# Where the decay broadcasts of an SSD scan are issued: from SyncE's DMA queue or from GpSimd's

## The chip, the cores and the metric

One core of one Trainium2 chip runs the whole program. The metric is the device time of one execution in microseconds (us); the kernel before has a median of 3172.28 us over three runs (3169.02 to 3177.87). Engines are called as in the profile: PE (TensorE), DVE (VectorE), ACT (ScalarE), POOL (GpSimd) and SP (SyncE). SP does no arithmetic here; in the kernel before it issues every DMA of the program.

## What is computed

The reference is one layer of a hybrid decoder for 2048 prompt tokens and 8 x 4 sample tokens, all in float32. A wide input projection feeds a depthwise convolution branch (31 taps) and a Mamba-2 SSD branch with 32 heads in 8 groups, chunks of 128 tokens and a state of 128; the branches are gated, projected, merged and projected again. What bears on the change is the SSD scan of one chunk:

```python
cum = jnp.cumsum(dtc * a, axis=2)                      # per head, over the chunk's 128 tokens
seg = cum[:, :, :, None] - cum[:, :, None]
decay = jnp.exp(jnp.where(mask, seg, -jnp.inf))        # 128 x 128 per head
cb = jnp.einsum('bcqgn,bckgn->bcqkg', cc, bc)
y_intra = jnp.einsum('bcqkgr,bckgrp->bcqgrp', cb[..., None] * decay, xdt)
...
y_inter = jnp.einsum('bcqgn,bcgrpn->bcqgrp', cc, h_starts) * jnp.exp(cum)[..., None]
```

For the difference `seg` on the chip, a token's cumulative sum has to stand on all 128 partitions (as a row) as well as in its own (as a column).

## The kernel before

Pass 1 (from line 900 on) does the input projection, the short convolutions, the 31-tap convolution and the SSD scan; pass 2 the output projections. Pass 1 goes over the tokens in two halves: the first has 1024 prompt tokens and the 32 sample tokens in three token blocks of 352, the second 1024 prompt tokens in two of 512. In each half the loop runs over 88 weight blocks of 1024 x 128. A float32 product is made of three matmuls (`mm3`, lines 134 to 140), so one weight block takes 24 matmuls per token block. The raw weights are loaded by `load_raw` (line 120, two buffers), split by ACT (line 130) and DVE (line 131) into two parts (three buffers each), and the products are accumulated in one of four PSUM tiles called `acc`, from which ACT or DVE empties them (`evac`, from line 759 on; line 768 for the blocks that feed the SSD branch).

The SSD work is put between these blocks. A unit is one group of four heads and one chunk: 8 groups x 9 units in the first half (the ninth holds the sample tokens) and 8 x 8 in the second. Each block-and-token-block step of the loop is a tick; a unit takes three ticks (two in places), and the small units of PE, ACT and DVE work are emitted at fixed ticks:

- `ssd_prefetch` (lines 594 to 606) takes one of five `se` tiles and loads into it the four heads' negated cumulative sums, broadcast to all 128 partitions (line 602; 128 x 4 x 128 floats, 256 KB; a ninth unit has three smaller loads, lines 602 and 606). Their source is the scratch tensor `d_cum`, written at line 535. It is called for the first three waiting units at the start of each unit (`prefetch(3)` in `tick_pre`), and for the first two of a group when that group is made.
- `ssd_seg` (lines 608 to 624) has ACT make the differences (line 621, four per unit) and the exponentials (line 623).
- `ssd_a_pe` and `ssd_a_vec` transpose and multiply on PE (lines 643 to 649) and DVE (lines 662 to 672); `ssd_b_pe` has PE read `se` for the last time (lines 706 and 709), and with that the tile is free.

POOL has small work only: the rows that a convolution needs from the block before it (lines 547, 548, 550, 859 to 862), the same for the 31-tap convolution (lines 876, 878, 891, 897), and a few sample-token steps (lines 655, 738, 875, 893).

The order of each engine's instructions is made by the tile framework, which takes the emitted order and the priorities given (`high_priority`); it may put an instruction earlier than it was emitted. Each engine, and each DMA-issuing queue, works its instructions off in that order: one that waits holds up all behind it.

Of the kernel before, what the change touches and what calls it, by code (L numbers as in the profile page):

```python
# [13 lines left out]
P = 128  # L14
# [73 lines left out]
class Kernel:  # L88
# [505 lines left out]
    def ssd_prefetch(self, un):  # L594
        if un is None:
            return
        half, g, c = un["half"], un["g"], un["c"]
        se = self.se_tile()
        un["se"] = se
        w, q0 = (P, c * P) if c < 8 else (NH, HALF)  # L600
        src = self.D["cum"][half][4 * g:4 * g + 4, q0:q0 + w]
        self.Q.dma_start(se[:, 0:4, :w], src.rearrange("(o h) q -> o h q", o=1).to_broadcast([P, 4, w]))
        if c < 8:
            return
        for r in range(2):
            self.Q.dma_start(se[64 * r:64 * r + 64, 4:6, :w], src[r:4:2].rearrange("(o h) q -> o h q", o=1).to_broadcast([64, 2, w]))

    def ssd_seg(self, un):

# [825 lines left out]
```

## Time and profile before

| what | value |
|---|---|
| median of three runs | 3172.28 us |
| the profiled execution | 3171.67 us, of which the profile's span is 3169.9 us |
| busy: PE, DVE, ACT, POOL | 3121.7, 2292.6, 1604.9, 145.3 us |
| DMA traffic | 392.92 MB, all of the program's own on one queue |
| DMA issues at lines 602 and 606 | 136 and 16, all on SP |

The span is the time from the first to the last instruction of the profiled execution. An engine's busy time leaves out waiting, and it leaves out the issuing of DMAs, which the profile keeps apart as the engine's sequencer (SPq, POOLq). A row of the waits names the instruction that waited, the one that released it, the total time, the number of times and the longest.

### The profile page before, as it was taken

The page shows a single profiled execution, that of the slowest core. Times are in us where ns is not written, and L with a number is a line of the kernel's source. Part 1 is how long each engine was busy: PE and PEld are TensorE (multiplying, and loading weights), DVE is VectorE, ACT ScalarE, POOL GpSimd, SP SyncE. Part 2 cuts the span into 40 slices and gives each one's busy share as a digit, 9 for nine tenths or more (in the row PEclk, how much of TensorE's full clock was granted, in tenths as well). Part 3 has the DMA queues.
Part 4 walks back from the last instruction along what each step waited for, and adds up shares of the span by engine and source line. Part 5 has one row for each costly group of instructions (what it writes and reads, how often), then busy time and mean ns, then how long its engine had stood idle before and what let it go on. Part 6 is the DMA issues. An engine that isn't in the chain of part 4 may idle for free.

```text
span 3169.9 us, 46695 instructions
## 1 busy us (share of the span) xinstructions
PE 3121.7 (98%) x18404; PEld 2801.7 (88%) x18404; DVE 2292.6 (72%) x3350; ACT 1604.9 (51%) x2515; POOL 145.3 (5%) x266
## 2 busy tenths in 40 slices
PE   7999999999999999999999999999999999999997
PEld 5999999999999999787778778777778999999997
DVE  5798796968779684477776957859557877777654
ACT  5765545545464533655644646456425553535332
POOL 0000010100001000000000000000000000000000
PEclk9999999999999999999999999999999999999999
DMA  5533333233333343222222222332327767666752
GB/s 215 158 96 107 84 94 94 80 105 90 89 86 93 99 137 119 79 60 87 83 74 78 81 81 79 102 93 67 97 92 251 228 198 248 210 227 214 229 162 88
DMA packets 235563, 392.92 MB, mean 124 GB/s; under 512 B 31568, under 2 KB 171280, under 8 KB 234320
## 3 DMA queue, kind: packets, MB, share of 16 engines
q1 hardware_dynamic: 235344, 389.94, 40.2%
q8 instruction: 144, 2.36, 0.3%
q14 instruction: 75, 0.61, 0.1%
HBM read 314.66 MB, written 75.22 MB: 123 GB/s over the span
## 4 chain that ended last, share of the span: by engine, by line
PE 92%; DMA 3%; DVE 3%; ACT 2%; issue 1%; SPq 0%; POOL 0%; ACTq 0%; DVEq 0%; POOLq 0%
PE acc L138 27%; PE acc L140 27%; PE acc L139 27%; PE ys L706 2%; PE ys L714 2%; DMA se<-d_cum 2%; PE ys L709 2%; PE tr L649 1%; DMA set<-xT 1%; PE tr L300 1%; PE tr L643 1%; PE tr L645 0%; PE tr L644 0%; ACT se L621 0%; DMA d_hx<-set 0%
## 5 line engine op out<-in xcount | busy, mean ns | idle before, releaser
L138 PE MATMUL acc<-hh,wh 128*128 128x352 f32 (+1 forms) x3520 | 1268.3, 360 | 0.0
L140 PE MATMUL acc<-hh,wl 128*128 128x352 f32 (+1 forms) x3520 | 1234.2, 351 | 1.0 <-DVE wl L131 1.0
L139 PE MATMUL acc<-hl,wh 128*128 128x352 f32 (+1 forms) x3520 | 1234.1, 351 | 0.0
L138 PEld LDWEIGHTS acc<-hh,wh 128*128 128x128 f32 x3520 | 661.5, 188 | 66.3 <-issue 3.9
L140 PEld LDWEIGHTS acc<-hh,wl 128*128 128x128 f32 x3520 | 661.1, 188 | 63.1 <-DVE wl L131 1.3
L139 PEld LDWEIGHTS acc<-hl,wh 128*128 128x128 f32 x3520 | 661.9, 188 | 60.5 <-issue 0.7
L584 DVE SCALAR_TENSOR_TENSOR acc<-u,cwh,acc 128x1024 f32<-128x1024 f32 x480 | 614.7, 1281 | 5.4
L130 ACT ACTIVATE wh<-wr 128x1024 fp32r<-128x1024 f32 x336 | 354.9, 1056 | 492.3 <-PE acc L139 455.8
L131 DVE TENSOR_TENSOR wl<-wr,wh 128x1024 fp32r<-128x1024 f32 x336 | 410.0, 1220 | 261.1 <-ACT wh L130 259.1
L621 ACT ACTIVATE se<-se,cum 128x128 f32<-128x128 f32 x544 | 176.9, 387 | 495.2 <-DMA se<-d_cum 461.0
L553 DVE SCALAR_TENSOR_TENSOR set<-raw,prm,set 128x1080 f32<-128x1080 f32 (+1 forms) x192 | 250.8, 1306 | 4.2 <-ACT set L545 2.9
L662 DVE TENSOR_TENSOR se<-se,set 128x512 f32<-128x512 f32 x120 | 82.4, 687 | 223.9 <-ACT se L623 220.9
L138 PE MATMUL acc<-yh,wh 128*128 128x416 f32 x640 | 226.2, 353 | 0.0
L140 PE MATMUL acc<-yh,wl 128*128 128x416 f32 x640 | 225.9, 353 | 0.0
L139 PE MATMUL acc<-yl,wh 128*128 128x416 f32 x640 | 223.4, 349 | 0.0
L623 ACT ACTIVATE se<-se 128x1024 f32<-128x1024 f32 (+1 forms) x136 | 135.1, 993 | 2.2 <-DMA se<-d_cum 0.2
L139 PEld LDWEIGHTS acc<-yl,wh 128*128 128x128 f32 x640 | 120.3, 188 | 2.9 <-issue 1.0
L623 ACT ACT_TABLE_LOAD x95 | 121.9, 1283 | 1.7
L138 PEld LDWEIGHTS acc<-yh,wh 128*128 128x128 f32 x640 | 120.1, 188 | 1.7 <-issue 1.0
L140 PEld LDWEIGHTS acc<-yh,wl 128*128 128x128 f32 x640 | 120.0, 187 | 0.8
L138 PE MATMUL acc<-mh,wh 128*128 128x416 f32 x320 | 114.1, 357 | 0.0
L706 PE MATMUL ys<-se,xd 128*64 128x128 f32 x1088 | 113.5, 282 | 0.0
(259 smaller groups left out, 3900.3 us busy)
## 6 DMA issues: line engine op xcount, KB each, us to landing
wr<-win SPq DMA_DIRECT2D x176, 512.0 KB
wr<-wso SPq DMA_DIRECT2D x80, 512.0 KB
se<-d_cum SPq DMA_DIRECT2D x128, 256.0 KB
wr<-wco SPq DMA_DIRECT2D x40, 512.0 KB
wr<-wo SPq DMA_DIRECT2D x40, 512.0 KB
yy<-d_y SPq DMA_DIRECT2D x40, 416.0 KB
tm<-d_m SPq DMA_DIRECT2D x80, 208.0 KB
d_m<-sp SPq DMA_DIRECT2D x48, 176.0 KB
```

Of the source, the lines that this page charges most:

```text
L130: self.S.activation(out=hi[:, :cols], in_=raw[:, :cols], func=AF.Copy)
L131: self.V.tensor_tensor(out=lo[:, :cols], in0=raw[:, :cols], in1=hi[:, :cols].bitcast(F32), op=ALU.subtract)
L138: self.PE.matmul(out, whi[:, w], hhi(k), start=first and k == 0, stop=False)
L139: self.PE.matmul(out, whi[:, w], hlo(k), start=False, stop=False)
L140: self.PE.matmul(out, wlo[:, w], hhi(k), start=False, stop=last and k == KD - 1)
L553: V.scalar_tensor_tensor(out=acc, in0=raw[:, k:k + L], scalar=w[:, k:k + 1], in1=acc, op0=ALU.mult, op1=ALU.add)
L584: V.scalar_tensor_tensor(out=a, in0=u[:, k:k + HALF], scalar=w[:, k:k + 1], in1=a, op0=ALU.mult, op1=ALU.add)
L621: self.S.activation(out=se[:, m + h, :w], in_=se[:, h, :w], func=AF.Relu, bias=col)
L623: self.S.activation(out=se[:, a:b, :w], in_=se[:, a:b, :w], func=AF.Exp, scale=-1.0)
L662: V.tensor_tensor(out=se[:, 0:4], in0=se[:, 0:4], in1=bc(un["C"], "p (o q) -> p o q", [P, 4, P], o=1), op=ALU.mult)
L706: PE.matmul(ys[64 * r:64 * r + 64, b * P:b * P + w], xd[:w, 2 * b + r, :], un["m"][:w, 2 * b + r, :w], start=True, stop=not inter)
L709: PE.matmul(ys[64 * r:64 * r + 64, b * P:b * P + w], self.hT[:, g, 64 * h:64 * h + 64], se[:, h, :], start=False, stop=True)
```

## The change

The three loads in `ssd_prefetch` are issued by `self.G` (`nc.gpsimd`, POOL) where `self.Q` (`nc.sync`, SP) issued them. Source, destination, size and callers stay as they are.

```diff
@@ -599,11 +599,11 @@
         un["se"] = se
         w, q0 = (P, c * P) if c < 8 else (NH, HALF)
         src = self.D["cum"][half][4 * g:4 * g + 4, q0:q0 + w]
-        self.Q.dma_start(se[:, 0:4, :w], src.rearrange("(o h) q -> o h q", o=1).to_broadcast([P, 4, w]))
+        self.G.dma_start(se[:, 0:4, :w], src.rearrange("(o h) q -> o h q", o=1).to_broadcast([P, 4, w]))
         if c < 8:
             return
         for r in range(2):
-            self.Q.dma_start(se[64 * r:64 * r + 64, 4:6, :w], src[r:4:2].rearrange("(o h) q -> o h q", o=1).to_broadcast([64, 2, w]))
+            self.G.dma_start(se[64 * r:64 * r + 64, 4:6, :w], src[r:4:2].rearrange("(o h) q -> o h q", o=1).to_broadcast([64, 2, w]))
```

## Rows read from the trace of the kernel before

**Rows 1.** The page, parts 0 and 1: span, busy time and share.

```profile
span 3169.9 us, 46695 instructions
PE 3121.7 (98%) x18404; PEld 2801.7 (88%) x18404; DVE 2292.6 (72%) x3350; ACT 1604.9 (51%) x2515; POOL 145.3 (5%) x266
```

**Rows 2.** Windows of the two SSD stretches: length, then busy time of each engine.

```profile
160.00:1200.00 1040.00, 1031.57 (x7217) 983.15 (x7216) 822.57 (x1308) 539.01 (x964) 74.39 (x155) 1.00 0.35 96
...
1320.00:2320.00 1000.00, 996.36 (x5306) 792.70 (x5305) 728.89 (x1035) 544.09 (x822) 51.64 (x71) 1.00 0.28 83
```

**Rows 3.** PE's longest wait in 160 to 1200 and in 1310 to 2310.

```profile
PE ys L744 <- DVE set L735: 5.5, 6, 1.1
...
PE ys L321 <- ACT sp L337: 2.0, 2, 1.5
```

**Rows 4.** The tile `se`: its loads (duration ns min/median/max, first and last start).

```profile
L602 SPq DMA_DIRECT2D se<-d_cum x136: 359/377/2904, 136.8 to 2290.8; - x136
...
L606 SPq DMA_DIRECT2D se<-d_cum x16: 599/640/1441, 218.1 to 1161.5; - x16
```

**Rows 5.** Waits of SP's queue, whole span: total, times, longest.

```profile
SPq L120 <- DVE wl L131: 1024.2, 268, 23.2
...
SPq L602 <- PE ys L709: 107.1, 59, 9.9
```

**Rows 6.** Timeline of SP's queue, first half: start, length, instruction.

```profile
442.34 0.39 SPq L602 DMA_DIRECT2D se<-d_cum  x1
...
468.46 0.36 SPq L602 DMA_DIRECT2D se<-d_cum  x1
...
536.98 9.88 SPq L602 DMA_DIRECT2D se<-d_cum  x2
...
580.58 0.90 SPq L602 DMA_DIRECT2D se<-d_cum  x1
```

**Rows 7.** Timeline of PE around one load, first half.

```profile
468.03 0.39 PE L709 MATMUL ys<-se,hT 128*64 128x128 f32 x4
...
472.56 0.32 PE L140 MATMUL acc<-hh,wl 128*128 128x352 f32 x1
...
486.39 0.32 PE L138 MATMUL acc<-hh,wh 128*128 128x352 f32 x1
...
504.35 0.41 PE L138 MATMUL acc<-hh,wh 128*128 128x352 f32 x1
```

**Rows 8.** Timeline of ACT behind the same load, first half (in brackets: idle before).

```profile
473.29 1.28 ACT L621 ACTIVATE se<-se,cum 128x128 f32<-128x128 f32 x4 [4.62 <-DMA se<-d_cum]
...
476.85 0.45 ACT L768 ACTIVATE raw<-acc 128x352 f32<-128x352 f32 x1
...
480.01 1.06 ACT L130 ACTIVATE wh<-wr 128x1024 fp32r<-128x1024 f32 x1
```

**Rows 9.** Waits of ACT, whole span: the one on these loads.

```profile
ACT se L621 <- DMA se<-d_cum: 461.0, 114, 8.6
```

**Rows 10.** POOL's groups of instructions: busy, mean ns, then idle before and releasers.

```profile
L860 POOL COPY raw<-sst 128x24 f32<-128x24 f32 x32 | 26.9, 843 | 41.2 <-DMA sst<-scv 41.2
...
L548 POOL COPY sst<-raw 128x24 f32<-128x24 f32 x32 | 8.7, 273 | 0.0
...
L859 POOL MEMSET raw<- 128x3 f32 x32 | 3.2, 101 | 172.4 <-DVE set L553 109.6 <-DVE acc L578 61.7 <-PE ys L744 1.1
...
L876 POOL MEMSET u<- 128x30 f32 x8 | 1.0, 123 | 119.0 <-DVE acc L584 119.0
```

**Rows 11.** Timelines of ACT and of PE, second half.

```profile
1801.20 0.58 ACT L768 ACTIVATE raw<-acc 128x512 f32<-128x512 f32 x1
...
1819.22 0.58 PE L138 MATMUL acc<-hh,wh 128*128 128x512 f32 x1
```

**Rows 12.** Timelines of SP's queue and of ACT, the first five loads.

```profile
136.81 5.10 SPq L602 DMA_DIRECT2D se<-d_cum  x5
...
155.58 0.98 ACT L621 ACTIVATE se<-se,cum 128x128 f32<-128x128 f32 x3
```

## The prediction

> **What bounds the kernel now.** I read the page's busy shares first, then the windows, the waits of PE, and last the timeline around one load. PE is busy for 3121.7 of 3169.9 us [rows 1]: it bounds the kernel, and a change can bring at most what PE stands idle, 48.2 us in all. The loads that move are issued between 136.8 and 2290.8 us [rows 4], so only the idle time in the two stretches of the SSD work counts: 1040.00 - 1031.57 = 8.4 us in the first half and 1000.00 - 996.36 = 3.6 us in the second [rows 2], together 12.0 us. Even this is not for the taking: PE's longest wait in the first half is on DVE's line 735 (5.5 us) and in the second on ACT's line 337 (2.0 us) [rows 3]; neither is a wait on a broadcast or on an emptied accumulator. The engine that does wait for the broadcasts is ACT: 461.0 us over 114 waits, 4.0 us each [rows 9]. But ACT is busy for about half of these stretches (539.01 of 1040) [rows 2], so its idle time is free as long as PE doesn't feel it.
>
> **How early the loads are.** One load shows the whole pattern. PE reads a tile of `se` for the last time at 468.03 us [rows 7], SP issues the next load into it at 468.46 [rows 6]: the load goes out as soon as a buffer is free. ACT, which has come to line 621, idles for 4.62 us and starts at 473.29 [rows 8], so issue to use is 4.83 us. The same buffer is loaded again five loads later, at 536.98 [rows 6], when PE is done with it; the reader sees that a unit's data lie there for 68 us. What follows from a late load is therefore not that this unit is late at PE, but that ACT, which works in order, stands longer in front of line 621 and holds up what is queued behind it: the emptying of an accumulator at 476.85 and a weight split at 480.01 [rows 8].
>
> **The cover.** The accumulator emptied at 476.85 was completed by PE's matmul at 472.56; PE comes to the same one four products later, at 486.39 [rows 7]. The emptying ends at 476.85 + 0.45 = 477.30, so ACT may be 486.39 - 477.30 = **9.1 us** later before PE waits. The split weights of 480.01 are first used at 504.35 [rows 7], 24 us later, so the accumulator decides. In the second half the emptying that ends at 1801.78 has until 1819.22 [rows 11], 17.4 us. The 9.1 us are the number on which this prediction stands.
>
> **What the change removes.** SP loses 136 issues of 0.377 us and 16 of 0.64 us [rows 4], 51.3 + 10.2 = 61.5 us, and the waits in front of them, the largest 107.1 us on PE's line 709 [rows 5]. What is queued behind them on SP are weight loads, and those wait for something else: 1024.2 us on DVE's line 131, which frees the raw buffer [rows 5]. So SP stands earlier at a wait that ends when it did. Gain: 0. The bound on the other side is the 12.0 us above.
>
> **What it adds.** POOL, busy for 145.3 us [rows 1], gets 152 DMA issues. No row of before shows a DMA issued by POOL, so I bound its price. From below: what SP takes, 0.38 us. From above: a load has 128 x 4 = 512 rows to describe, and POOL's plain copy of 24 elements per partition takes 273 ns, 11.4 ns each (line 548, [rows 10]); 512 x 11.4 = 5.8 us. Between them I take 3.5 us, an estimate nearer the upper end, because the work is done element by element on POOL as that copy is. Issue to use then grows by 3.5 - 0.4 = 3.1 us, from 4.8 to 7.9 us (bounds: 0 to 5.4 us more). All of these are under 9.1 us: cost at PE, 0. POOL's own time rises by 136 x 3.5 + 16 x 0.9 = 490 us (16 loads of a quarter of the rows), to some 635 us of 3170, spread over 2150 us: it doesn't become the bound. POOL's halo copies and memsets now stand behind a broadcast for up to 5.8 us; the first emptying of the next block waits for them, and it has the same kind of cover. If that cover were gone, each us past it would be paid once per unit, 136 times.
>
> **Where loads come in a burst.** At the start of the first half five loads are issued in 5.10 us, and the last of their differences begin at 155.58 [rows 12]. On POOL at 3.5 us each the fifth is issued by 136.81 + 17.5 = 154.3 and lands 4.4 us later, at 158.7: ACT is 3.1 us late, covered. At 5.8 us each it lands at 136.81 + 29.0 + 4.4 = 170.2, 14.6 us late and 5.5 us past the cover; the second half begins with a burst too, so the upper bound of this term is 11.0 us.
>
> **A rule against the change.** POOL's copy of line 860 takes 843 ns where line 548, of the same shape, takes 273; its memset of line 859, which only writes, takes 101 ns [rows 10]. POOL's reads thus stand behind something and its writes don't. The Trainium skill, SBUF — State Buffer, section "SBUF: two separate sides", says that a DMA issued from GpSimd has its descriptors written by GpSimd, which is locked out while DVE runs an operation that takes both ports of the shared pair. By that rule the broadcasts would be late for as long as DVE holds the ports, and it is a rival below; by the rows on memsets alone, nothing is added. I side with the rows, as writing descriptors is nearest to them.
>
> **Sum.** 0 gained, 0 paid. The profiled execution took 3171.67 us (3169.9 of span and 1.8 around it), 0.6 us under the median of 3172.28, so the sum stands for the median as well: 3172.3 us. With the bounds the forecast's own case goes from 3172 to 3183.
>
> **The rivals.**
> 1. *A broadcast is caught behind a waiting POOL instruction (slower).* The place: the memset of line 876 waits for the 31-tap convolution to free its buffer, 119.0 us over 8 groups, 14.9 us each [rows 10]. A broadcast queued behind it, where SP's queue let it pass, would be 14.9 + 3.1 = 18.0 us late, 8.9 us more than the cover; once per group in the first half that is 8 x 8.9 = 71 us: 3243 us. It decides from 9.1 us of lateness on. For it: POOL works in order, and these waits are real. Against it: in the queue of before the loads leave within half a us of the buffer's release, and the order of POOL's queue is made by the same planner.
> 2. *Writing the descriptors is held up by DVE (slower by much).* The pace of line 860 is 843 / 24 = 35 ns per element, 18.0 us for 512 rows. A group of nine units takes 580.58 - 442.34 = 138.2 us [rows 6] and its loads would take 9 x 18.0 = 162 us on POOL, which then bounds the kernel: 8 x 23.8 = 190 us in the first half alone, at least 3362 us. It decides from 138.2 / 9 = 15.4 us per load on. For it: line 860. Against it: line 859.
> 3. *SP's relief reaches PE (faster).* All idle time of PE in the two stretches goes: 3172.3 - 12.0 = 3160 us. Against it: rows 3 name DVE and ACT, not SP.
>
> **How the numbers follow.** A measurement of this kernel tells 0.3%, 9.5 us, from no change. Chances: the forecast 0.69, rival 1 0.17, rival 2 0.06, rival 3 0.08. The forecast's own case lies within 9.5 us but for the end of its upper bound, 0.02, which I count as slower. So faster 0.08, same 0.67, slower 0.25. The range 3164 to 3200 holds the forecast's case, part of rival 3, and rival 1 where only three of the groups are caught (3 x 8.9 = 27 us); it leaves out rival 2, the rest of rival 1 and the larger gains, together less than 2 in 10.
>
> **What would show it.** Right: `se<-d_cum` among POOL's issues, SP's waits at line 602 gone, ACT's wait at line 621 up from 4.0 us to about 7 each, PE's busy time at 3121 us and its idle time in the two stretches still about 12 us with no wait on `acc` or `se`. Wrong in the cost: a broadcast that takes POOL over 5.8 us. Wrong in the mechanism: PE waiting at line 138 for an accumulator that ACT empties late (rival 1 if POOL's line 876 precedes it, rival 2 if POOL is busy without a break), or PE's idle time shrinking with the order of the queues as it was (rival 3).

## The result and the profile after

The kernel with the change takes 3202.69 us (median of 4 runs, 3201.34 to 3204.91); the kernel before, on the same chip, takes 3174.72 us (4 runs). The ratio is 1.0092, with a 95% interval of 1.008 to 1.0104: 28 us slower, above the upper end of the range. (Ratios here and below are estimated over all runs of both kernels, so they are not exactly the quotient of two medians. 0.1% is 3.2 us.)

The page of the kernel after, parts 0, 1 and 3 (in part 3: packets, MB, share of the span of 16 DMA engines); it answers to [rows 1]:

```profile
span 3199.9 us, 46748 instructions
...
PE 3126.2 (98%) x18404; PEld 2805.6 (88%) x18404; DVE 2288.3 (72%) x3350; ACT 1615.9 (50%) x2523; POOL 246.7 (8%) x418
...
q1 hardware_dynamic: 161232, 355.59, 34.3%
q0 software_dynamic: 11008, 34.35, 8.3%
```

POOL's busy time rises by 101.4 us (on POOL, unlike on SP, the profile counts an issue as busy time; those at lines 602 and 606 take 104.2 + 9.6 us), and PE needs 4.5 us more for the same 18404 matmuls. The other 25.5 of the 30.0 us that the span grows by are idle time of PE. The windows of the two SSD stretches say where; they answer to [rows 2], with the same columns:

```profile
160.00:1200.00 1040.00, 1008.28 (x7032) 961.17 (x7031) 815.95 (x1292) 540.75 (x966) 131.31 (x239) 0.99 0.37 94
1320.00:2320.00 1000.00, 993.70 (x5249) 790.85 (x5248) 713.74 (x1029) 557.85 (x825) 93.58 (x138) 1.00 0.33 81
```

PE stands idle for 1040.00 - 1008.28 = 31.7 us in the first half (8.4 before) and 6.3 us in the second (3.6). The three largest waits of PE in 160 to 1200 us of the kernel after, against [rows 3]:

```profile
PE ys L166 <- DVE sq L159: 17.8, 1, 17.8
PE ys L744 <- DVE set L735: 9.1, 6, 1.6
PE ys L833 <- DVE sp L822: 2.6, 1, 2.6
```

One single wait is over half of the loss, and it is not at an SSD instruction: line 166 is a matmul of the second half's input norm (`x_norm` and `x_rstd`, from line 147 on), which DVE's line 159 feeds. The loads themselves look harmless. All instructions of line 602 in the kernel after (first row: duration ns min/median/max, first and last start), and ACT's wait on them, which answers to [rows 9]:

```profile
L602 POOL DMA_DIRECT2D se<-d_cum x136: 747/755/950, 137.5 to 2320.5; - x136
...
DMA to landing us min/median/max: 3.6/5.3/10.8
```

```profile
ACT se L621 <- DMA se<-d_cum: 489.2, 111, 9.5
```

POOL needs 0.76 us for a load, and half of them land within 5.3 us. ACT's wait has grown by 28 us over the whole span, 0.4 us a time. What the medians hide is the start of the first half. POOL's timeline in the kernel after:

```profile
137.46 0.95 POOL L602 DMA_DIRECT2D se<-d_cum  x1 [26.25 <-PE acc L140]
142.92 0.76 POOL L602 DMA_DIRECT2D se<-d_cum  x1 [4.51 <-issue]
148.39 0.75 POOL L602 DMA_DIRECT2D se<-d_cum  x1 [4.70 <-issue]
159.45 0.76 POOL L602 DMA_DIRECT2D se<-d_cum  x1 [10.31 <-issue]
166.22 0.75 POOL L602 DMA_DIRECT2D se<-d_cum  x1 [6.01 <-issue]
```

POOL issues a load, stands, and issues the next, and the rows name no semaphore for its standing ("issue"). SP put the same five out within 5.10 us [rows 12], so neither the tiles nor the sums are missing. ACT's timeline of the kernel after, over the same time, with the norm's first instruction, line 153, at its end:

```profile
159.17 0.40 ACT L621 ACTIVATE se<-se,cum 128x128 f32<-128x128 f32 x1 [8.91 <-DMA se<-d_cum]
...
165.94 0.40 ACT L621 ACTIVATE se<-se,cum 128x128 f32<-128x128 f32 x1 [4.54 <-DMA se<-d_cum]
...
171.44 0.40 ACT L621 ACTIVATE se<-se,cum 128x128 f32<-128x128 f32 x1 [3.28 <-DMA se<-d_cum]
...
176.59 1.25 ACT L153 ACTIVATE set<-set 128x1280 f32<-128x1280 f32 x1
```

Each of these waits ends when a load lands, and 0.28 us after it POOL issues the next (159.17 and 159.45, 165.94 and 166.22): POOL has one load on its way at a time. All four later issues come 0.3 us after the landing of the load before (142.61, 148.08, 159.15 and 165.91 us in the trace). The third load takes longest, 10.8 us: from 148.4 to 154.0 us the DMA engines work for SP's queue alone (90.3% of their time), and the load's first packet moves 5.9 us after its issue, where that of the first two moved after 1.5 to 1.8 us. In the kernel before ACT's line 153 began at 160.84, and PE came to line 166 with 1.54 us to wait:

```profile
160.84 1.27 ACT L153 ACTIVATE set<-set 128x1280 f32<-128x1280 f32 x1 [1.26 <-DMA set<-xT]
...
168.25 0.81 PE L166 MATMUL ys<-sq,cst 128*128 128x320 f32 x2 [1.54 <-DVE sq L159]
```

In the kernel after line 153 is 176.59 - 160.84 = 15.8 us later, and so is all that follows from it, on PE in the end:

```profile
184.21 1.43 PE L166 MATMUL ys<-sq,cst 128*128 128x320 f32 x2 [17.76 <-DVE sq L159]
```

The stop costs more than its length. PE's windows around it in the kernel after (length, PE busy, granted clock, DMA share, GB/s):

```profile
166.00:184.20 18.20, 0.45 (x3) 0.66 0.31 57
184.20:200.00 15.80, 15.79 (x88) 0.85 0.36 85
```

Behind the stop PE is busy without a break, but at a granted clock of 0.85, a mean over time at 2.4 and at 1.2 GHz, and gets 88 matmuls done where the kernel before, from the same matmul on (168.24 to 184.04 us), did 101 at 1.00. That is 0.15 x 15.8 = 2.4 us, on top of 17.76 - 1.54 = 16.2 us.

### The profile page after: what moved, and what is told of

Same layout as the page of the kernel before. It is cut to its first block, busy times and chain, and to the rows that moved or that the text cites. A ratio compares the mean times of both kernels' runs of the same rounds, so it can differ in the third digit from the quotient of the medians.

```text
span 3199.9 us, 46748 instructions
## 1 busy us (share of the span) xinstructions
PE 3126.2 (98%) x18404; PEld 2805.6 (88%) x18404; DVE 2288.3 (72%) x3350; ACT 1615.9 (50%) x2523; POOL 246.7 (8%) x418
## 3 DMA queue, kind: packets, MB, share of 16 engines
q1 hardware_dynamic: 161232, 355.59, 34.3%
q0 software_dynamic: 11008, 34.35, 8.3%
## 4 chain that ended last, share of the span: by engine, by line
PE 76%; DVE 7%; issue 7%; DMA 6%; ACT 4%; POOL 0%; SPq 0%; POOLq 0%; ACTq 0%; DVEq 0%
PE acc L140 22%; PE acc L138 22%; PE acc L139 22%; DMA se<-d_cum 4%; PE ys L706 2%; PE ys L714 2%; DVE acc L584 1%; PE ys L709 1%; ACT se L621 1%; DVE wl L131 1%; DVE set L553 1%; PE tr L649 1%; PE tr L300 1%; ACT wh L130 1%; ACT se L623 1%
## 5 line engine op out<-in xcount | busy, mean ns | idle before, releaser
L602 POOL DMA_DIRECT2D se<-d_cum x136 | 104.2, 766 | 880.2 <-PE ys L709 399.8
```

What stands on the lines that cost most here:

```text
L602: self.G.dma_start(se[:, 0:4, :w], src.rearrange("(o h) q -> o h q", o=1).to_broadcast([P, 4, w]))
```

## The experiments

**What moves besides the loads.** The framework orders the instructions anew for each kernel, and moving loads changes that order. Taking line, operation and tiles of each instruction in turn from the traces (table loads left out), the kernel after and e1, e1c, e2 and e7 below have one and the same order on PE, DVE and ACT; so have the kernel before, e3 and e7c. Between the two groups some 150 of ACT's 2277 instructions and some 100 of DVE's 3350 stand elsewhere, the first of them at 223 us, behind the opening; on PE a few matmuls do, at six places between 408 and 1101 us and between 2025 and 2076 us. The kernels e4, e5, e6, e8, e9 and e10 each have an order of their own. A comparison inside a group shows the loads alone; any other shows the loads and the order together.

**The opening: five loads, and why one at a time.** Two kernels move only the five opening loads (the first half's group 0, units 0 to 4): one takes them out of the change, one makes them the whole change.

```diff
 # e2_open_sp, in the kernel after
+(self.Q if half == 0 and g == 0 and c < 5 else self.G).dma_start(se[:, 0:4, :w], ...
 # e3_open_pool, in the kernel before
+(self.G if half == 0 and g == 0 and c < 5 else self.Q).dma_start(se[:, 0:4, :w], ...
```

> The changed kernel with only the first five broadcasts (first half, group 0, units 0 to 4) issued by SP again; the other 131 and the 16 small ones stay on POOL. Theory A (the opening is the loss): PE's wait at line 166 is under 4 us, about 20 us of the loss go, 3180 to 3185 us; what is left, 5 to 10 us, is spread over the groups. Rival C (each broadcast pays, by landing later or by holding up POOL): the loss stays spread, 3195 us or more.

> The kernel before with only the first five broadcasts (first half, group 0, units 0 to 4) issued by POOL. Theory A: these five cost by themselves about 20 us (PE idle 17 us at line 166, and some 3 us in which the granted clock comes back): 3190 to 3196 us. Rival C (each broadcast pays): five of 136 cost about 1 us, 3173 to 3178 us.

The other pair asks what keeps POOL from issuing. The kernel is built with `dynamic_dma_scratch_size=1024` (line 1430), taken here as the space for the descriptors (the written orders) of POOL's loads; one kernel doubles it, and as the room for that comes from moving a small tile (`cT`) to another pool, a control moves the tile alone.

```diff
 # e1_ring2048, in the kernel after; e1c_ring1024: the first edit alone
-            cT = pp.tile([P, KD, 9], F32, name="cT")
+            cT = self.spp.tile([P, TB], F32, tag="sp", name="cT")[:, :72].rearrange("p (k c) -> p k c", k=KD)
-    nc = bacc.Bacc("TRN2", ..., dynamic_dma_scratch_size=1024)
+    nc = bacc.Bacc("TRN2", ..., dynamic_dma_scratch_size=2048)
```

> The changed kernel with twice the descriptor space for POOL's DMAs (dynamic_dma_scratch_size 2048 in place of 1024; the small tile cT is taken from another pool to make room). Theory A: the loss comes from the opening five broadcasts, each of which left POOL only when the one before it had landed, because the space holds the descriptors of one load. Then with twice the space at least two loads go out without such a wait, the five are issued within 20 us (34 in the changed kernel), PE's wait at line 166 falls from 17.8 us to under 8, and the time is near 3185 us. Rival B: POOL's queue takes one load at a time whatever the space; the issues stay 5 to 11 us apart, the wait at line 166 stays, 3203 us.

> The control for the run with twice the space: the changed kernel with cT taken from the other pool and the descriptor space as it was (1024). Both theories: as the changed kernel, 3200 to 3206 us, PE's wait at line 166 between 16 and 20 us.

| kernel | median us (runs) | ratio to before, 95% | PE's wait at line 166 |
|---|---|---|---|
| after, opening on SP (e2) | 3189.81 (5) | 1.0039 [1.0027, 1.0051] | 1.6 us |
| before, opening on POOL (e3) | 3193.61 (5) | 1.0055 [1.0043, 1.0067] | 17.5 us |
| after, 2048 bytes (e1) | 3188.96 (6) | 1.0040 [1.0026, 1.0053] | 2.1 us |
| after, tile moved (e1c) | 3205.03 (5) | 1.0082 [1.0069, 1.0095] | 17.1 us |

POOL's timeline with 2048 bytes:

```profile
137.03 2.45 POOL L602 DMA_DIRECT2D se<-d_cum  x3 [25.99 <-PE acc L140]
142.67 0.76 POOL L602 DMA_DIRECT2D se<-d_cum  x1 [3.19 <-issue]
143.77 0.75 POOL L602 DMA_DIRECT2D se<-d_cum  x1 [0.34 <-issue]
```

Three loads now leave together, and the fourth and fifth leave 0.31 us after the first and the second have landed (142.36 and 143.46). So this setting decides how many loads of 512 rows are on their way: one with 1024 bytes, three with 2048. That it is room for descriptors that runs out was supposed, not shown, and why twice the number gives three is open. Five loads alone (e3) make 0.55% = 17.5 us with every order as in the kernel before, and the two kernels that mend the opening, in ways that have nothing else in common and with every order as in the kernel after, both bring the wait at line 166 back to 2 us. The opening is settled. It is not everything: e1 and e2 stay 12 to 13 us above the kernel before, where near 3185 us (e1) and 3180 to 3185 us (e2) had been expected.

**Does line 166 decide, or would PE have stopped anyway?** A delay of the norm by six ticks, with the change and without.

```diff
-            for _ in range(8 if tb else 1):
+            for _ in range((1, 8, 14)[tb]):
```

> The changed kernel with the third part of the token normalisation for the second half (hx_stage) begun six ticks later, so that PE's matmul of line 166 no longer stands right behind the opening burst. If the opening costs what it does because that one matmul had no time to spare, while the emptying of accumulators has some 9 us: PE stands 6 to 10 us in the opening, in front of a matmul into an accumulator, instead of 17 us at line 166, and the kernel takes 7 to 12 us less than the changed one, 3190 to 3196 us. If the accumulators have no more time to spare than that matmul, PE stands 15 us or more all the same, 3200 us or more.

> The control: the kernel before with the same later start of that part. Both readings: within 5 us of the kernel before, 3172 to 3182 us, as PE waits for neither there.

With the change 3206.15 us (5 runs), 1.0092 [1.0078, 1.0106]; without it 3177.17 (11), 1.0004 [0.9995, 1.0013]. The number alone looks like the second reading, but the traces say that nothing was tried. In the delayed kernel with the change ACT's line 153 begins at 176.62 us (176.59 in the kernel after), and both kernels have the orders of those that they were made from: the later emission left the norm at its old place in the queues. Whether PE would have come to another late operand behind line 166 stays open.

**The other 12 us: which loads?** Three kernels: the change without the opening and the ninth units, the ninth units alone, and the second half alone.

```diff
 # e4_open_ninth_sp, in the kernel after (line 606 on self.Q too)
+(self.Q if c == 8 or half == 0 and g == 0 and c < 5 else self.G).dma_start(...
 # e5_ninth_pool, in the kernel before (line 606 on self.G too)
+(self.G if c == 8 else self.Q).dma_start(...
 # e6_second_pool, in the kernel before
+(self.G if half == 1 else self.Q).dma_start(...
```

> The changed kernel with the first five broadcasts and the three small ones of each ninth (sample) unit issued by SP; the other 123 stay on POOL. With the opening on SP alone, 12 us of loss were left, of which some 11 came in steps of 1 to 3 us where one group gives way to the next in the first half and some 5 near 2050 to 2130 us. Theory N: the ninth unit's three small loads on POOL make these steps; then the first half's steps go, 3181 to 3184 us. Rival O: any load on POOL does it there (where POOL's queue or the planner's order puts it); the steps stay, 3187 to 3191 us.

> The kernel before with only the ninth units' loads (8 large-strided ones of 64 KB and 16 of 16 KB) issued by POOL. Theory N: the steps between the groups of the first half appear, 8 to 11 us, 3183 to 3189 us. Rival O: nothing to be told from the kernel before, 3174 to 3180 us.

> The kernel before with the 64 broadcasts of the second half alone issued by POOL. The theory that the loss lies in the opening and at the group ends of the first half: this costs 3 to 6 us (the drift seen near 2050 to 2130 us), 3177 to 3184 us, and its own opening burst (five loads, one at a time) costs PE nothing, since no matmul waits on work queued behind them there. Rival C (each broadcast pays alike): 64 of 136 cost half of the 29 us, 3190 us or more.

With the opening and the ninth units on SP (e4) the time is 3186.81 us (5 runs), 1.0035 [1.0022, 1.0048]; with the ninth units alone on POOL (e5) 3175.58 (11), 1.0006 [0.9997, 1.0015]. The ninth units are not it. The second half's 64 loads (e6) make 3181.45 (11), 1.0011 [1.0002, 1.002], so 3.5 us, although its own five opening loads go out one at a time as well (POOL's issues at 1318.20, 1324.37, 1329.58): no wait of PE stands behind them. Its loss lies in one place: from 1320 to 2000 us and from 2140 to 2320 us PE has no idle time. PE's windows between, in e6 and, below, in the kernel before:

```profile
2000.00:2140.00 140.00, 132.38 (x770) 0.99 0.36 94
```

```profile
2000.00:2140.00 140.00, 136.36 (x803) 1.00 0.32 99
```

136.36 - 132.38 = 4.0 us, in the waits at lines 315 and 321, on the vectors for the gates that are made there. What the loads have to do with these is not shown: in e6 the order of PE itself differs there, and e7c, with the loads and the order of the kernel before, stands idle for 5.0 us in the same window (134.96 of 140.00 busy).

That leaves some 8 us in the first half. Unit by unit, the kernel with opening and ninth units on SP loses them in steps near a group's end. The first and largest is at 290 to 310 us; PE's windows there, in this kernel and then in the kernel before:

```profile
290.00:300.00 10.00, 7.05 (x48) 0.88 0.50 153
300.00:310.00 10.00, 10.00 (x60) 0.77 0.53 139
```

```profile
290.00:300.00 10.00, 9.34 (x67) 1.00 0.46 153
300.00:310.00 10.00, 10.00 (x78) 1.00 0.49 117
```

The load that ACT waits for ahead of this is that of unit 4 of group 1. So the last three kernels go by that: units 3 and 4 of the later groups alone, everything but these, and this one load.

```diff
 # e8_c34_pool, in the kernel before
+(self.G if half == 0 and g > 0 and c in (3, 4) else self.Q).dma_start(...
 # e9_c34_sp, in the kernel after (line 606 on self.Q too)
+(self.Q if c == 8 or half == 0 and (c in (3, 4) or g == 0 and c < 5) else self.G).dma_start(...
 # e10_one_pool, in the kernel before
+(self.G if half == 0 and g == 1 and c == 4 else self.Q).dma_start(...
```

> The kernel before, with only the loads of units 3 and 4 of the groups 1 to 7 of the first half on POOL (14 of 136). Theory S (what is left without the opening is paid at a few loads, those at a group's end, where data written and read for the ninth unit share the DMA engines and where DVE's queue has no slack): 3180 to 3184 us, PE's wait at line 833 near 297 us 2.5 to 3.0 us (0.7 before), its waits at line 744 in 200 to 1200 about 9 us in sum (5.5 before). Rival E (every load costs its share, 8 us over 59 loads of the first half): 14 x 0.14 = 1.9, so 3177 us, and line 744 at 6.5 us or less.

> As the kernel with the opening five and the ninth units' loads on SP, and units 3 and 4 of all groups of the first half on SP as well; POOL keeps 45 loads of the first half and 64 of the second. Theory S: only the second half's 3 to 4 us and at most 2 more remain, 3177 to 3181 us, and PE's wait at line 833 near 297 us is back at about 0.7 us. Rival E: 45 of the 59 loads are still on POOL, so 8 x 45/59 = 6.1 us of the first half remain: 3175 + 6.1 + 3.5 = 3185 us.

> The kernel before, with one load on POOL, that of unit 4 of group 1 of the first half (issued by SP at 280 us before). Theory S: it lands about 2 us later (7 us after its issue for 5), ACT's next split and emptying are 2 to 3 us later, PE's wait at line 833 near 297 us grows from 0.7 to 2 to 3 us, and the granted clock of 290 to 310 us falls below 1.00; 3177 to 3180 us. Rival E: one load costs nothing that can be seen, line 833 waits under 1 us and the clock stays at 1.00.

| kernel | median us (runs) | ratio to before, 95% |
|---|---|---|
| before, 14 loads on POOL (e8) | 3187.52 (6) | 1.0033 [1.0021, 1.0044] |
| after, those, opening and ninth on SP (e9) | 3181.75 (11) | 1.0018 [1.0009, 1.0027] |
| before, one load on POOL (e10) | 3180.22 (11) | 1.0015 [1.0006, 1.0024] |

One load of 256 KB on another queue, with what its move does to the order, costs 0.15% = 4.8 us (1.9 to 7.6). Its way to PE can be followed, in the kernel with the one load on POOL, on SP, POOL, ACT, DVE and PE:

```profile
282.62 3.12 SPq L751 DMA_DIRECT2D o_hs<-acc  x2
...
282.74 0.95 POOL L602 DMA_DIRECT2D se<-d_cum  x1 [0.30 <-POOL set L738]
...
289.96 0.40 ACT L621 ACTIVATE se<-se,cum 128x128 f32<-128x128 f32 x1 [5.74 <-PE acc L140]
290.27 1.04 ACT L130 ACTIVATE wh<-wr 128x1024 fp32r<-128x1024 f32 x1
291.22 0.45 ACT L777 ACTIVATE sp<-acc 128x352 f32<-128x352 f32 x1
...
291.35 1.22 DVE L131 TENSOR_TENSOR wl<-wr,wh 128x1024 fp32r<-128x1024 f32 x1 [4.58 <-ACT wh L130]
292.49 0.52 DVE L814 TENSOR_TENSOR set<-set,sp 128x352 f32<-128x352 f32 x1
...
299.97 0.52 DVE L822 TENSOR_TENSOR sp<-sq 128x352 f32<-128x352 f32 x1
...
300.64 0.52 PE L833 MATMUL ys<-sp,cst 128*32 128x88 f32 x8 [3.03 <-DVE sp L822]
```

The same instructions in the kernel before:

```profile
280.23 0.37 SPq L602 DMA_DIRECT2D se<-d_cum  x1
280.65 2.88 SPq L751 DMA_DIRECT2D o_hs<-acc  x2
...
285.22 0.70 ACT L621 ACTIVATE se<-se,cum 128x128 f32<-128x128 f32 x2 [3.22 <-DMA se<-d_cum]
285.83 0.44 ACT L777 ACTIVATE sp<-acc 128x352 f32<-128x352 f32 x1
...
286.37 0.53 DVE L814 TENSOR_TENSOR set<-set,sp 128x352 f32<-128x352 f32 x1 [2.61 <-ACT sp L777]
...
295.38 0.51 DVE L822 TENSOR_TENSOR sp<-sq 128x352 f32<-128x352 f32 x1
...
296.04 0.36 PE L833 MATMUL ys<-sp,cst 128*32 128x88 f32 x8 [0.66 <-DVE acc L581]
```

This execution had been 2.23 us behind the other since before (ACT's differences of the unit ahead start at 278.80 against 276.57), which has to come off every difference. The load leaves 0.3 us later (282.74 against SP's 280.23), is there 7.1 us after its issue, where SP's was used after 5.0, and ACT's line 621 is 289.96 - 285.22 - 2.23 = 2.5 us late. (The row names PE's line 140 as what ACT waited for; the load landed at 282.74 + 7.1 = 289.8, so it was the load.) Why it lands late can be seen as well. SP issued it ahead of the two stores of line 751; POOL issues it 0.12 us behind the first of them, and from 282.7 to 285.0 us the DMA engines move the stores and nothing of POOL's queue (packets, MB, share of 16 engines):

```profile
q1 hardware_dynamic: 144, 0.52, 59.4%
```

Behind line 621 the order is not that of the kernel before: ACT has line 130 ahead of line 777, and DVE line 131 ahead of line 814. So line 814 is 3.9 us late. At line 822 this is made up: in the old order, with the kernel before's distances, it would have begun at 289.96 + 295.38 - 285.22 = 300.12 us, an estimate, and it began at 299.97. It is 2.4 us late, and PE's wait grows by 3.03 - 0.66 = 2.4; the late load is enough for that, without the order. The DVE rows between show why the rest is not made up: from 286.4 to 309.0 us of the kernel before DVE is busy for 22.60 of 22.60 us. What DVE begins late there, it ends late. Behind the wait the clock falls (one row of PE's windows, same kernel), 0.17 x 10 = 1.7 us more:

```profile
300.00:310.00 10.00, 9.36 (x67) 0.83 0.48 154
```

The 14 loads of e8 make 0.33% = 10.5 us (6.7 to 14.0), at least as much as is left in the first half (11.1 of e4 less 3.5, so 7.6) and more than theory S had put down; rival E's 1.9 us are out. PE's waits in 190 to 1200 us of this kernel, to which come 2.2 us at line 695 (0.7 before):

```profile
PE ys L744 <- DVE set L735: 8.8, 5, 2.1
PE ys L833 <- DVE sp L822: 2.9, 1, 2.9
PE ys L706 <- ACT sp L836: 2.6, 1, 2.6
```

With e9 line 833 is back at 0.8 us, and 5.7 us remain of the whole change, 3.5 of them the second half's: 3181.75 us is just above theory S's range and short of rival E's 3185. Line 744 still waits for 8.0 us (5.5 before). This is no sign of the loads: in e5, which costs nothing that can be told, it waits for 7.5. In e4, e6, e8 and e9 the order moved with the loads, so that the late load is followed to PE at one place only, 290 us; for the rest of these 12 us no run separates the loads from the order.

The parts add up: opening 17.5 (e3), 14 loads at the groups' ends 10.5 (e8), second half 3.5 (e6), together 31.5 us, against 0.92% = 29.2 us (25.4 to 33.0) for the change. The plainer sum, of the five loads alone and of all but these: 17.5 (e3) + 12.4 (e2) = 29.9 us. None of the versions is faster than the kernel before.

## Why the prediction was wrong

**What held.** PE bounds the kernel and nothing was gained from SP's relief: SP stands at line 120 in place of line 602 (1218.6 us for 1024.2 in [rows 5]), as foreseen. In the steady part the loads cost what was said, or less: 5.3 us to landing against the 4.8 of before, where 7.9 was expected, and 4.4 us for each of ACT's waits at line 621, where about 7 was. The cover of 9.1 us held on its own path: PE has no wait at line 138 for an accumulator that ACT empties late.

**The term "where loads come in a burst" failed in its mechanism.** It put the price of a load down as POOL's own work, 0.38 to 5.8 us, and let five loads follow each other at that pace. POOL's work is 0.76 us, near the lower bound. What spaces the loads is that the next one waits until the last has landed, 5.5 to 11 us apart. With the program's first five loads this makes the larger part of the loss, 17.5 of 29.2 us. By chance the upper bound came out at the right lateness (14.6 us forecast, 15.8 us seen at ACT's line 153), but it was set aside as the far end of the range and charged only with what lay past the cover, 5.5 us. Line 1430 with its 1024 bytes stood in the code, and the question how many loads it lets out at once was not asked.

**The step "the cover" failed in its reach.** 9.1 us was worked out for one path (ACT empties an accumulator) at one place (468 to 486 us), and then used for 136 loads. Two paths had none, or less than the delay. One is the norm: PE's wait at line 166 is there in the kernel before, 1.54 us long, which says that its operand arrives late already and that every further us is paid in full: 15.8 us of lateness, 16.2 us of wait. The other is line 833 at 296 us, with 0.66 us of wait before and 3.03 in e10: DVE's queue is full there, DVE waits for ACT, and ACT waits for the load. The prediction looked at the longest wait alone, DVE's line 735 in [rows 3], read it as "not a wait on a broadcast" and passed on; a wait names the last link of a chain only, and the short ones were not followed back. Whether line 735's waits hang on the loads too is not shown.

**The order was taken as given.** The sum has no term for the new order that the framework makes when a load changes its queue, and the section on the change speaks of the loads alone. Some 12 us (e2) come with loads and order together, and how they divide stays open.

**The clock was left out.** A wait can be followed by a stretch at a lower granted clock: it cost 2.4 us behind line 166 and 1.7 us behind line 833 in the kernel with one load on POOL. It need not: with 14 loads on POOL line 833 waited 2.9 us and the clock of the next 10 us was 1.00.

**The rivals.** Rival 1 came small and at another line, and PE did not feel it. POOL's line 876 waits less than before (56.0 us, 10.0 the longest, for the 119.0 of [rows 10], seven waits each time), but five loads of the second half stand behind line 878, which waits for DVE, and leave 2.0 to 3.5 us later after PE's last read of their buffer than in the kernel before, under the cover. One of them, on POOL in the kernel after:

```profile
2252.26 1.80 POOL L878 COPY u<-chalo 128x30 f32<-128x30 f32 x1 [4.20 <-DVE acc L584]
2254.00 0.76 POOL L602 DMA_DIRECT2D se<-d_cum  x1
```

PE has no wait at line 138. Rival 2: the groups of POOL's instructions in the kernel after (busy, mean ns, idle before), against [rows 10]:

```profile
L602 POOL DMA_DIRECT2D se<-d_cum x136 | 104.2, 766 | 880.2 <-PE ys L709 399.8 <-DVE wl L131 121.3 <-PE ys L714 116.1
L860 POOL COPY raw<-sst 128x24 f32<-128x24 f32 x32 | 26.9, 844 | 40.7 <-DMA sst<-scv 40.5 <-issue 0.2
```

Line 860 is as slow as it was (that POOL's reads are held up was a poor reading of it: line 548 reads too, and takes 273 ns in [rows 10]), and the issues take 747 to 950 ns each, while DVE is busy for 72% of the time. The Trainium skill, SBUF — State Buffer, section "SBUF: two separate sides", has GpSimd locked out of writing descriptors while DVE runs certain operations; no issue of this kernel shows it. Rival 3: PE's idle time grew. The point "wrong in the mechanism" looked for an accumulator at line 138; the waits came at lines 166, 833 and 744.

## What to carry to other kernels

Before a load is moved to GpSimd's queue, ask how many loads it must have on its way at once, and find the place where the kernel issues several together: a mean price per load says nothing about a burst, and a setting of the program can be the limit, as line 1430 is here. A cover holds for the path and the place where it was read; so look through PE's short waits in the kernel before (1.5 us at line 166, 0.7 at 833), follow each back to the load, and count a path that hangs on it as having no cover at all. Compare the order of the instructions in the two traces before a difference is put down to the edit: where loads move, the framework may move the rest. Look where an engine that is idle on average is busy without a break, since there it passes a delay on in full.

## What the runs showed that was not expected

- With 1024 bytes in line 1430 POOL has one load of 512 rows on its way, with 2048 bytes three, and its standing between them is named "issue", not a semaphore.
- The same bytes cost the DMA engines more from POOL's queue: 34.35 MB take 8.3% of their time there, while the queue that lost them fell from 389.94 MB and 40.2% to 355.59 MB and 34.3%, so by 5.9 points (of a span 30.0 us longer); in 11008 packets where that queue lost 235344 - 161232 = 74112. The Trainium skill, DMA: Bandwidth & Descriptors, section "Issuing engines are not separate DMA queues", says that DMAs share the same engines whoever starts them, and that another issuer saves only the time to initiate them. Here the issue took 0.38 us on SP and takes 0.76 us on POOL, and what SP saved reached nothing.
- The median load from POOL lands 0.5 us later after its issue than the one load of [rows 6, 8] was used (5.3 for 4.8), and the one of unit 4 of group 1 is there 2.1 us later (7.1 for 5.0). Late data go with other traffic: of the 136 loads of the kernel after, 31 have their first packet more than 2.4 us after the issue, and from 1 us after the issue until then other queues held the 16 DMA engines for 67% of the time or more. That DVE was in the way is not needed for any of them.
